# A hybrid trunk in split float32r products: first products on x as loaded, one weight tile of the opening instead of two, and an earlier low part ahead of the up tiles

## The chip, the cores and the metric

One core of one Trainium2 chip. The metric is the device time of one execution in microseconds (us); below, the median of three runs is given beside the one execution that the hardware profiler recorded. Engines: PE (TensorE, the products), DVE (VectorE), ACT (ScalarE), POOL (GpSimd) and SP, whose queue issues most transfers.

## The reference, cut to what matters

One layer on 512 rows of 1024 columns:

```
u    = x * rsqrt(mean(x*x, axis=-1) + eps) * g          # rmsnorm, g = ln1_g
proj = u @ w_in       # q, k, v, pool_in, z, xbc, dt_raw, gate_pre
y_b  = pool_mixer(pool_in): per channel, windows w = 2, 4, 8, 16 by group
       (cumsum(p)[t] - cumsum(p)[t-w]) / min(t+1, w) - p[t], then a product
x    = x + (gates * (attention, pool, state-space branches)) @ w_o
x    = x + conv_ffn(rmsnorm(x, ln2_g))                  # w_up, conv, silu, w_down
out  = rmsnorm(x, final_g)
```

The factor rsqrt(...) is one number per row of x, so it can be applied to x before a product or to the rows of the result after it.

## The kernel before, in words

**Products.** Every large product is made of three float32r products: each operand is held as a high part (rounded to float32r) and a low part (what the rounding left), and high by high (HH), high by low (HL) and low by high (LH) are added in one PSUM bank. `mm3` (its product is L239) writes them. A weight tile is 1024 rows by 256 columns: `fetch` loads it, `cast` (L195, ACT) writes the high part `wh`, `low` (L217, DVE) the low part `wl`. For the activations the two parts are `uh` and `ul`, transposed: eight tiles k of 128 columns of x, each 128 partitions by 512 rows of x. The rows of x come in four blocks of 128 (tb = 0 to 3), loaded in two halves each.

**Order of work.** Everything is issued in program order on each engine. `program()` yields a list of jobs, one weight tile each: first the eight pool column blocks (four tiles, called w0 to w3 here), then the v columns, q and k, and so on to `w_o`, the up tiles and the down tiles. Before the body of job n, `prepare` issues low(n+1), cast(n+2) and fetch(n+3); a job marked `late` calls `prepare` itself, inside its body. `step()` advances generators in the lists `running` and `waiting`, one piece of side work at each call.

**The opening** (L1814 to L1952) is written out by hand. PE runs 12 products of ones (L1833) while x is on its way. For row blocks 0 and 1, ACT and DVE form sums of squares (L442), then a chain of small operations (L1897 to L1902) ends in a diagonal matrix that holds the row factors (L1903); PE multiplies each 128x128 block of x by it (L1891), which transposes and norms in one product. ACT (L1862) and DVE (L1863) read the PSUM result, multiply by g and write `uh` and `ul` in pieces of 128x256. Row blocks 2 and 3 are normed in place (L1927, L1929) and transposed against the unit matrix `eye` later (L1940). `begin` (L1866 to L1881) does w0 and w1 in two passes: rows 0 to 255 for both tiles, then rows 256 to 511 for both, 192 products of 256 columns (L1874) in all. Between the passes stand the transposes and a transpose of small constants, `colp` (L508). From w2 on a job does 48 products of 512 columns.

**Pool evacuation** (`pool_evac`, L896 to L919). For each of the eight pool column blocks ACT copies PSUM to `pu`, POOL adds shifted copies until the window is reached (L904 to L907), and two steps later DVE subtracts `pu` (L913), ACT rounds (L915) and DVE writes the low part (L916).

**Into the FFN.** The last `w_o` job, `four`, is late: its `prepare`, which holds the low part of up tile 0, the cast of up tile 1 and the fetch of up tile 2, is put on `late_split` and run only after row block 3 of the second norm has been set up (L1325). The first two up tiles run `up_jobs.opening` (L1532 to L1562): rows 0 to 255 first, HH, HL, then transposes of the next normed block (L454), the low part of the next tile, then LH (all L1543).

## Time and profile before

| | |
|---|---|
| runs | 1013.71, 1014.82, 1015.12 us; median 1014.82 |
| profiled execution | 1014.97 us |
| its span | 1013.2 us |
| PE busy | 1001.3 us (99%), 5360 matmul records |
| DVE busy | 733.4 us (72%) |
| ACT busy | 529.9 us (52%) |
| POOL busy | 156.2 us (15%) |
| last PE product ends | 1005.85 us |

The busy time of an engine is counted inside the span; the profiled execution is 1.8 us longer than its span. Idle time of an engine counts only where another waits for it, and with PE busy 99% of the span there is very little idle time on PE: 4.58 us ahead of its last product. In rows of the trace a group reads as start, length, engine, line, operation, output<-inputs, shape, count, and in brackets the idle time ahead of it and who ended it.

### The profile page before, as it was taken

To read this page: it belongs to the slowest core of one execution; us is meant where nothing else is said; L and a number is where in the kernel's file an instruction comes from. 1 tells how busy PE (TensorE), PEld (TensorE's weight loads), DVE (VectorE), ACT (ScalarE), POOL (GpSimd) and SP (SyncE) were. 2 spreads that over 40 slices of the span, in tenths; PEclk is the share of its full clock that TensorE was granted. 3 is DMA by queue.
4 is the path that set the end of the run, shared out by engine and by line. 5 is a ranking of instruction groups with operands and counts; after the bars stand their busy time and mean duration, and the time that the engine had idled before them with its cause. 6 is when DMAs were issued, how large, how long until landed. Compare 5 with 4: busy or idle time off the path is not lost.

```text
span 1013.2 us, 13676 instructions
## 1 busy us (share of the span) xinstructions
PE 1001.3 (99%) x5360; PEld 853.5 (84%) x5360; DVE 733.4 (72%) x923; ACT 529.9 (52%) x904; POOL 156.2 (15%) x143
## 2 busy tenths in 40 slices
PE   8999999999999999999999999999999999999997
PEld 8898878999988888888888888898888888888885
DVE  6564758577767655776789888768778768685877
ACT  5433556464436566788576246554444434443455
POOL 1680010110000000000044501302111100121132
PEclk9999999999999999999999999999999999999999
DMA  7334270654352435552254754232252134542573
GB/s 238 89 102 139 84 208 5 167 169 144 99 166 76 116 94 146 142 132 62 83 149 119 222 188 87 83 123 87 89 202 84 44 115 149 181 115 73 146 181 110
DMA packets 117584, 126.76 MB, mean 125 GB/s; under 512 B 6772, under 2 KB 96439, under 8 KB 117520
## 3 DMA queue, kind: packets, MB, share of 16 engines
q1 hardware_dynamic: 111887, 116.39, 37.0%
q0 software_dynamic: 5040, 8.65, 5.5%
q8 instruction: 42, 0.69, 0.3%
q10 hardware_dynamic: 592, 0.86, 0.3%
q14 instruction: 23, 0.18, 0.1%
HBM read 121.30 MB, written 3.00 MB: 123 GB/s over the span
## 4 chain that ended last, share of the span: by engine, by line
PE 93%; DVE 3%; issue 1%; DMA 1%; ACT 1%; POOL 0%; ACTq 0%; POOLq 0%
PE pa L239 36%; PE pu L239 23%; PE pb L239 8%; PE pqk L239 6%; PE pd L239 6%; PE pq L239 3%; PE pa L1874 2%; PE ps L781 1%; PE ppw L239 1%; PE po L829 1%; DVE wl L217 1%; PE pt L815 1%; PE py L1114 1%; PE pu L1543 1%; DMA xin<-in_x_dram 1%
## 5 line engine op out<-in xcount | busy, mean ns | idle before, releaser
L217 DVE TENSOR_TENSOR wl<-raw,wh 128x2048 fp32r<-128x2048 f32 (+3 forms) x86 | 205.9, 2394 | 42.3 <-ACT wh L195 33.9
L195 ACT CAST wh<-raw 128x1024 fp32r<-128x1024 f32 (+3 forms) x169 | 169.8, 1022 | 48.6 <-DVE raw L362 17.8
L1440 DVE SCALAR_TENSOR_TENSOR hc<-pu,fcol,hc 128x510 f32<-128x510 f32 x88 | 65.8, 748 | 53.1 <-ACT hc L1437 51.4
L239 PE MATMUL pa<-uh,wh 128*128 128x512 f32 (+1 forms) x368 | 88.8, 381 | 0.0
L239 PE MATMUL pa<-ul,wh 128*128 128x512 f32 (+1 forms) x368 | 86.8, 375 | 0.0
L239 PE MATMUL pa<-uh,wl 128*128 128x512 f32 (+1 forms) x368 | 86.8, 375 | 0.0
L239 PE MATMUL pu<-uh,wh 128*128 128x512 f32 (+1 forms) x352 | 83.5, 379 | 0.0
L239 PE MATMUL pu<-uh,wl 128*128 128x512 f32 (+1 forms) x352 | 83.5, 379 | 0.0
L239 PE MATMUL pu<-ul,wh 128*128 128x512 f32 (+1 forms) x352 | 83.5, 379 | 0.0
L239 PEld LDWEIGHTS pa<-ul,wh 128*128 128x128 f32 x368 | 66.7, 188 | 12.6
L239 PEld LDWEIGHTS pa<-uh,wl 128*128 128x128 f32 x368 | 66.7, 188 | 12.5
L239 PEld LDWEIGHTS pa<-uh,wh 128*128 128x128 f32 x368 | 65.3, 188 | 11.8
L239 PEld LDWEIGHTS pu<-uh,wl 128*128 128x128 f32 x352 | 64.2, 188 | 12.5
L239 PEld LDWEIGHTS pu<-ul,wh 128*128 128x128 f32 x352 | 64.2, 188 | 12.5
L239 PEld LDWEIGHTS pu<-uh,wh 128*128 128x128 f32 x352 | 64.1, 188 | 12.4
L1445 POOL TENSOR_TENSOR hc<-hc 128x512 f32<-128x512 f32 x22 | 29.9, 1361 | 279.3 <-DVE hc L1440 243.3
L1437 ACT ACTIVATE hc<-pu,fcol,fcol 128x512 f32<-128x512 f32 x40 | 31.2, 780 | 75.0 <-PE pu L239 75.0
L217 DVE TENSOR_TENSOR wl<-w,wh 128x2048 fp32r<-128x2048 f32 (+1 forms) x26 | 54.3, 2087 | 10.2 <-issue 4.6
L195 ACT CAST wh<-w 128x1024 fp32r<-128x1024 f32 (+1 forms) x52 | 47.2, 950 | 9.8 <-DMA w<-in_ffn_w_down_dram 5.0
L803 ACT ACTIVATE sb<-sb,nmls 128x128 f32<-128x128 f32 (+1 forms) x72 | 30.0, 418 | 31.4 <-DVE nmls L800 20.8
L1097 POOL TENSOR_TENSOR st<-st,dts 128x512 f32<-128x512 f32 x4 | 4.2, 1052 | 226.1 <-ACT st L1105 165.7
L1442 ACT ACTIVATE hc<-hc 128x512 f32<-128x512 f32 x22 | 13.9, 632 | 40.3 <-DVE hc L1440 40.3
(443 smaller groups left out, 1969.4 us busy)
## 6 DMA issues: line engine op xcount, KB each, us to landing
raw<-in_w_in_dram SPq DMA_DIRECT2D x24, 1024.0 KB, 5.5
raw<-in_ffn_w_up_dram SPq DMA_DIRECT2D x22, 1024.0 KB, 5.2
raw<-in_w_in_dram SPq DMA_DIRECT2D x14, 512.0 KB
raw<-in_w_in_dram SPq DMA_DIRECT2D x8, 768.0 KB, 7.4
raw<-in_ffn_w_down_dram SPq DMA_DIRECT2D x6, 1024.0 KB, 5.1
raw<-in_w_b_dram SPq DMA_DIRECT2D x4, 1024.0 KB, 5.3
al<-ad SPq DMA_DIRECT2D x16, 256.0 KB, 6.4
raw<-in_w_c_dram SPq DMA_DIRECT2D x4, 1024.0 KB, 7.7
```

The lines of the kernel that those rows point to most:

```text
L195: (other.tensor_copy if other and i else act.copy)(job.high[:, :, o], job.raw[:, :, o])
L217: (eng or dve).tensor_tensor(l[:, :, o], job.raw[:, :, o], h[:, :, o].bitcast(F32), OP.subtract)
L239: pe.matmul(ps, l, r, start=first and n == 0, stop=last and n == total - 1, skip_group_check=onto)
L781: pe.matmul(pss[i][:, o:o + w * P], q[r, n * P:(n + 1) * P], k[r, kb * P:(kb + w) * P], start=True, stop=True)
L803: act.activation(sb[:, off:off + w * P], sb[:, off:off + w * P], AF.Exp, bias=nm[:, n, h:h + 1], accum_out=ls[:, n, h:h + 1])
L815: pe.transpose(pt[:, o:o + P], sb[:, o:o + P], eye)
L829: pe.matmul(po[DH * hh:DH * hh + DH, n * P:(n + 1) * P], V[g, kb + i][:, (2 * c + hh) * DH:(2 * c + hh + 1) * DH], probs[2 * c + hh, nb][: ...
L1437: act.activation(t, ps, AF.Identity, bias=ff["c1"][:, ff["b"] + m:ff["b"] + m + 1], scale=fw(2, m))
L1440: dve.scalar_tensor_tensor(t[:, sh:], ps[:, :S - sh], fw(k, m), t[:, sh:], OP.mult, OP.add)
L1442: act.activation(t, t, AF.Silu)
L1445: pool.tensor_tensor(a, a, t, OP.mult)
L1874: pe.matmul(first[2 * n + j][:, lo:hi], a[:, k, j * P:(j + 1) * P], b[:, k, lo:hi], start=a is wh and b is uh and k == 0, stop=a is wl and ...
```

## The change

- x is transposed as it was loaded (PE against `eye`, L1902), without the row factor. ACT (L1906) and DVE (L1907) multiply by g and write high and low parts `xh`, `xl` in 32 pieces each of 128x128. Row block 1 goes to three PSUM banks (`uT1`, `first[2]`, `first[1]`) instead of sharing those of row block 0.
- Ten products of ones stand ahead (`WARM`), seven more (`STILL`) behind the transposes of row block 1.
- Only w0 is done by hand, again in passes of 256 rows: 96 products (L1918). Its high part is cast by DVE and ACT, its low part made by POOL. w1 is an ordinary job of 48 products of 512 columns (L239).
- The row factors of all four blocks are formed during this, as a column `rcol`; PE transposes it (L1992), DVE copies it out, and it goes to DRAM and comes back as a tile `rows` with the 512 factors in every partition.
- `pool_evac` runs on DVE: a multiply by `rows` (L929), two running sums with `tensor_tensor_scan` (the first w columns at L931; then at L932 each new element adds p[t] and subtracts p[t-w]), the factor for the first w elements (L933); the difference and the low part follow four and five steps later (L938, L942). POOL no longer adds shifted copies.
- The normed `uh`, `ul` of the later jobs come from `xf`, the sum of both parts of x, times `rows` (POOL, L642), rounded by ACT (L643) and subtracted by DVE (L649). The v columns use `xh` and `xl` and ACT multiplies their results by `rcol`. Four additions on DVE (L408) are not needed any more.
- x, `eye`, g and w0 are loaded in another order; `turn()` and `parts_of_bias()` are moved three and four steps into the job loop.
- `four` is no longer late, so low(up tile 0), cast(up tile 1) and fetch(up tile 2) go ahead of its body. In the opening of up tile 0, LH now goes ahead of the transposes and of low(up tile 1); for up tile 1 the order stays.

```diff
-        f = []
-        for k in (2 * p, 2 * p + 1):
-            f.append(T("uf"))
-            dve.tensor_tensor(f[-1], uh[:, k, :].bitcast(F32), ul[:, k, :].bitcast(F32), OP.add)
+        if p < 2:
+            f = [xf[2 * p], xf[2 * p + 1]]
...
+    def normed():
+        for k in range(0, KD, 2):
+            for i in (k, k + 1):
+                pool.tensor_tensor(xf[i], xf[i], rows["r"], OP.mult)
+                act.copy(uh[:, i, :], xf[i])
+            yield
+        yield
+        for k in range(0, KD, 2):
+            yield
+            for i in (k, k + 1):
+                dve.tensor_sub(ul[:, i, :], xf[i], uh[:, i, :].bitcast(F32))
...
-            act.copy(t[:, :384], ps[:, :384])
+            act.mul(t[:, :384], ps[:, :384], rcol[:, tb:tb + 1])
...
-        return jobs_b(parts, 384 + extra, lambda k, tb: uh[:, k, tb * P:(tb + 1) * P],
-                      lambda k, tb: ul[:, k, tb * P:(tb + 1) * P], KD, evac)
+        return jobs_b(parts, 384 + extra, lambda k, tb: xh[k][:, tb * P:(tb + 1) * P],
+                      lambda k, tb: xl[k][:, tb * P:(tb + 1) * P], KD, evac)
...
-        act.copy(u, ps)
-        cur, sh = u, 1
-        while sh < w:
-            nxt = T("psw")
-            pool.tensor_tensor(nxt[:, sh:], cur[:, sh:], cur[:, :S - sh], OP.add)
-            pool.tensor_copy(nxt[:, :sh], cur[:, :sh])
-            cur, sh = nxt, sh * 2
-        pool.tensor_tensor(cur[:, :w], cur[:, :w], ramp[:, g, :w], OP.mult)
+        dve.tensor_tensor(u, ps, rows["r"], OP.mult)
+        cur = T("psw")
+        dve.tensor_tensor_scan(cur[:, :w], ones.bitcast(F32)[:, :w], u[:, :w], 0.0, OP.mult, OP.add)
+        dve.tensor_tensor_scan(cur[:, w:], u[:, w:], u[:, :S - w], cur[:, w - 1:w], OP.add, OP.subtract)
+        dve.tensor_tensor(cur[:, :w], cur[:, :w], ramp[:, g, :w], OP.mult)
         def later():
+            for _ in range(4):
+                yield
+            dve.scalar_tensor_tensor(cur, cur, 1.0 / w, u, OP.mult, OP.subtract)
+            dh, dl = T("pdh", F32R), T("pdl", F32R)
+            act.copy(dh, cur)
             yield
-            yield
-            d = T("pd")
-            dve.scalar_tensor_tensor(d, cur, 1.0 / w, u, OP.mult, OP.subtract)
-            dh, dl = T("pdh", F32R), T("pdl", F32R)
-            act.copy(dh, d)
-            dve.tensor_sub(dl, d, dh.bitcast(F32))
+            dve.tensor_sub(dl, cur, dh.bitcast(F32))
...
                 late.append(rest())
-                for _ in late_split.pop(0):
-                    pass
...
-        four.late, inner = True, four.body
-        def body(ws):
-            late_split.append(four.prepare(later=True))
-            inner(ws)
-        four.body = body
...
                 product(ws[0], uh2, 0)
                 product(ws[0], ul2, 1)
+                if half == 0:
+                    product(ws[1], uh2, 2)
                 next(late.pop(0), None)
                 next(rest[0], None)
-                product(ws[1], uh2, 2)
+                if half:
+                    product(ws[1], uh2, 2)
...
-        yield from jobs_a(w_in, C_POOL, 8, uhk, ulk, KD, pool_evac)
+        yield from jobs_a(w_in, C_POOL, 8, xhk, xlk, KD, pool_evac)
...
-    load_x(0, (sp, act))
-    act.dma_start(eye, c_eye)
-    load_x(1, (sp, act))
     act.dma_start(g8[:KD, :P], ln1_g[0].rearrange("(k p) -> k p", p=P))
+    sp.dma_start(eye, c_eye)
+    load_x(0, (act, sp))
...
+    first = [MM("pa") for _ in range(3)]
...
+    load_x(1)
+    load_w0(0, 0, 8)
+    load_w0(1, 0, 8)
     load_x(2)
     load_x(3)
+    fetch(w1)
...
-    for tb in range(2):
-        s0, s1, v, sq, r, rt = (small(n, [P, 1]) for n in ("s0", "s1", "v", "sq", "r", "rt"))
-        squares(act, xin[tb, 0], s0)
-        squares(dve, xin[tb, 1], s1)
-        dve.tensor_scalar(v, s0, 1.0 / D, EPS, OP.mult, OP.add)
...
-        if tb == 0:
-            for k in range(KD):
-                turn_scale(0, k)
+    def block(tb, k):
+        if tb == 1:
+            return (uT1, first[2], first[1])[k % 3][:, (k // 3 + 1) * P:(k // 3 + 2) * P]
+        return bank(k)[:, tb % 2 * P:tb % 2 * P + P]
+    def turned(tb):
+        if tb % 2 == 0:
+            banks[:] = [SM("uT") for _ in range(4)]
+        for k in range(KD):
+            pe.transpose(block(tb, k), xin[tb, k // 4][:, (k % 4) * P:(k % 4 + 1) * P], eye)
+    def split_x(tb, k):
+        c = slice(tb * P, (tb + 1) * P)
+        act.mul(xh[k][:, c], block(tb, k), g1[:, k:k + 1])
+        dve.scalar_tensor_tensor(xl[k][:, c], block(tb, k), g1[:, k:k + 1],
+                                 xh[k][:, c].bitcast(F32), OP.mult, OP.subtract)
...
+    warm_up(WARM)
     pe.transpose(first[2][:, :KD], g8[:KD, :P], eye[:KD, :KD])
+    turned(0)
     dve.tensor_copy(g1, first[2][:, :KD])
...
-    cast(weights[0], 2, other=dve)
-    low(weights[0], 2, pool)
     for k in range(KD):
-        turn_scale(1, k % 2 * 4 + k // 2)
+        split_x(0, k)
+    turned(1)
     for k in range(KD):
-        turned(k, 0, bank(k))
...
-    ss = row_squares(2, small("ss", [P, 4]), 2)
-    next(parts)
-    r = rstd_of(ss, 2, D)
-    for tb in (2, 3):
-        for h in range(2):
-            t = xin[tb, h]
-            if h:
-                dve.tensor_scalar(t, t, r[:, tb - 2:tb - 1], None, OP.mult)
-            else:
-                act.mul(t, t, r[:, tb - 2:tb - 1])
-    next(parts)
-    begin(0, 0, 256)
...
-    begin(1, 0, 256, turns)
-    turn()
-    parts_of_bias()
+        if k == 2:
+            for k0 in (0, 4):
+                dve.tensor_copy(h0[part(0, k0, k0 + 4)], raw0[part(0, k0, k0 + 4)])
+            low0(0, 0, KD)
+        split_x(1, k)
+    warm_up(STILL, 0)
+    group(0, (HH,), 0, 256)
+    group(0, (HL,), 0, 256)
+    for k0 in (0, 4):
+        act.copy(h0[part(1, k0, k0 + 4)], raw0[part(1, k0, k0 + 4)])
+    low0(1, 0, KD)
+    half_squares(act, 0, 0)
+    half_squares(act, 1, 0)
+    half_squares(dve, 0, 1)
+    group(1, (HH,), 0, 256)
+    turned(2)
+    for k in range(KD):
+        split_x(2, k)
+    group(1, (HL,), 0, 256)
+    group(0, (LH,), 0, 256)
+    half_squares(act, 2, 0)
+    half_squares(dve, 1, 1)
+    for k in range(KD):
+        pool.tensor_tensor(xf[k][:, :256], xh[k][:, :256].bitcast(F32), xl[k][:, :256].bitcast(F32),
+                           OP.add)
+    turned(3)
+    for k in range(KD):
+        split_x(3, k)
+    group(1, (LH,), 0, 256)
     fetch(weights[2])
+    half_squares(act, 3, 0)
+    half_squares(act, 3, 1)
+    half_squares(dve, 2, 1)
+    both_high(256, S, (0, 1))
+    group(0, (LH,), 256, S)
+    group(1, (LH,), 256, S)
+    w1.high = whp.tile([P, KD, 256], F32R, name="wh", tag="wh")
+    dve.tensor_tensor(ss[:, :4], ss[:, :4], ss[:, 4:], OP.add)
+    r = rstd_of(ss[:, :4], 4, D)
+    for j in range(2):
+        act.copy(w1.high[:, :, j * P:(j + 1) * P], w1.raw[:, :, j * P:(j + 1) * P])
+    dve.tensor_copy(rcol, r)
+    pe.transpose(first[2][:4, :P], rcol, eye)
+    rt, rd = T("rowsT"), dram.tile([S], F32, name="rows")
+    dve.tensor_copy(rt[:4, :P], first[2][:4, :P])
+    rows["r"] = T("rows")
+    sp.dma_start(rd.rearrange("(t p) -> t p", p=P), rt[:4, :P])
+    sp.dma_start(rows["r"], rd.partition_broadcast(P))
+    low(w1, 2)
+    cast(weights[2], 2)
     fetch(weights[3])
-    begin(0, 256, S)
-    cast(weights[2])
+    for k in range(KD):
+        act.mul(xf[k][:, 256:], bank(k), g1[:, k:k + 1])
     low(weights[2])
-    begin(1, 256, S)
-    cast(weights[3])
-    fetch(weights[4])
+    running.append(after(3, columns_of(turn)))
+    running.append(after(4, columns_of(parts_of_bias)))
+    for j in range(2):
+        pool_evac(j, first[j])
+        step()
+    running.append(normed())
...
-        if n >= 2:
+        if n >= 1:
...
-                    if n + 1 < len(weights):
+                    if n + 1 < len(weights) and not weights[n + 1].split:
...
-WARM = 12
+WARM, STILL = 10, 7
```

What PE runs first, before; `uT` is the PSUM bank of transposed x, `pa` a bank of products:

```order
L1833 MATMUL pa<-ones 128x128 x12
L1891 MATMUL uT<-diag,xin 128x128 x8
L1907 MATMUL pa<-eye,g_109 128x8
L1891 MATMUL uT<-diag,xin 128x128 x8
L1874 MATMUL pa<-uh,wh 128x256 x6
L1874 MATMUL pa<-ul,wh 128x256 x2
```

And after, with `uT_123` the new bank and `xh`, `xl` the parts of x as loaded:

```order
L1854 MATMUL pa<-ones 128x128 x10
L1943 MATMUL pa<-eye,g_110 128x8
L1902 MATMUL uT<-eye,xin 128x128 x8
L1902 MATMUL uT_123<-eye,xin 128x128
L1902 MATMUL pa<-eye,xin 128x128 x2
...
L1854 MATMUL pa<-ones 128x128 x7
L1918 MATMUL pa<-xh,wh 128x256 x8
L1918 MATMUL pa<-xl,wh 128x256 x8
L1918 MATMUL pa<-xh,wh 128x256 x8
L1902 MATMUL uT<-eye,xin 128x128 x8
L1918 MATMUL pa<-xl,wh 128x256 x8
L1918 MATMUL pa<-xh,wl 128x256 x8
```

The ones and the transposes follow one another without the products with `diag`, eight products of w0 run in one group (HH of the first 128 columns) ahead of any low part, and the transposes of row blocks 2 and 3 stand as two groups of eight among the products.

DVE, from the low part of w3 on, before (`pd` and `pdl` are the window difference and its low part):

```order
L217 TENSOR_TENSOR wl<-raw,wh 128x2048
L913 SCALAR_TENSOR_TENSOR pd<-psw,pu 128x512
L916 TENSOR_TENSOR pdl<-pd,pdh 128x512
L913 SCALAR_TENSOR_TENSOR pd<-psw,pu 128x512
L916 TENSOR_TENSOR pdl<-pd,pdh 128x512
```

And after, from the row factors to the first evacuated block (`psw` holds the running sum; order prints a scan as SCALAR_TENSOR_TENSOR):

```order
L1991 COPY rcol<-r_446 128x4
L1994 COPY rowsT<-pa 4x128
L217 TENSOR_TENSOR wl<-raw,wh 128x8x128 x2
L217 TENSOR_TENSOR wl<-raw,wh 128x2048
L929 TENSOR_TENSOR pu<-pa,rows 128x512
L931 SCALAR_TENSOR_TENSOR psw<-ones,pu 128x2
L932 SCALAR_TENSOR_TENSOR psw<-pu,psw 128x510
L933 TENSOR_TENSOR psw<-psw,ramp 128x2
```

DVE now evacuates each pool block itself, behind the low parts of w1 and w2, with one multiply on PSUM, two scans and a small factor.

PE at the opening of the up tiles, before (`pu` is the bank of the up products, `u_5939` a row block of the second norm):

```order
L1543 MATMUL pu<-uh_5804,wh 128x256 x16
L1543 MATMUL pu<-ul_5805,wh 128x256 x16
L454 MATMUL uT<-eye,u_5939 128x128 x4
L454 MATMUL uT<-eye,u_5940 128x128 x4
L1543 MATMUL pu<-uh_5804,wl 128x256 x16
L1543 MATMUL pu<-uh_5804,wh 128x256 x16
```

And after:

```order
L1560 MATMUL pu<-uh_5788,wh 128x256 x16
L1560 MATMUL pu<-ul_5789,wh 128x256 x16
L1560 MATMUL pu<-uh_5788,wl 128x256 x16
L457 MATMUL uT<-eye,u_5930 128x128 x4
L457 MATMUL uT<-eye,u_5931 128x128 x4
L1560 MATMUL pu<-uh_5788,wh 128x256 x16
L1560 MATMUL pu<-ul_5789,wh 128x256 x16
```

The 16 products on `wl` now stand ahead of the two groups of transposes. On DVE at the same place, before, with `x` the residual row blocks 2 and 3, `va`, `vo` scalars of their norm and `wl` the low part of up tile 0:

```order
L1352 TENSOR_TENSOR x_5529<-x_5529,pb 128x512
L1304 TENSOR_SCALAR va_102<-so_101 128x1
L1305 TENSOR_SCALAR vo_103<-va_102 128x1
...
L479 SCALAR_TENSOR_TENSOR u_5939<-x_5529,rt,grow 128x512
L1352 TENSOR_TENSOR x_5531<-x_5531,pb 128x512
L1304 TENSOR_SCALAR va_105<-so_104 128x1
L1305 TENSOR_SCALAR vo_106<-va_105 128x1
L217 TENSOR_TENSOR wl<-raw,wh 128x2048
```

And after:

```order
L217 TENSOR_TENSOR wl<-raw,wh 128x2048
L1376 TENSOR_TENSOR x_5513<-x_5513,pb 128x512
L1330 TENSOR_SCALAR va_103<-so_102 128x1
L1331 TENSOR_SCALAR vo_104<-va_103 128x1
...
L482 SCALAR_TENSOR_TENSOR u_5930<-x_5513,rt,grow 128x512
L1376 TENSOR_TENSOR x_5515<-x_5515,pb 128x512
L1330 TENSOR_SCALAR va_106<-so_105 128x1
L1331 TENSOR_SCALAR vo_107<-va_106 128x1
```

The low part of up tile 0 went from behind the second addition to ahead of the first.

More of the change, by code (lines that the diff above doesn't have):

```diff
@@ new lines, in columns_of, with mm, group @@
+    def columns_of(turn):
+        turn()
+        return
+        yield
+    opened = set()
+    def mm(j, w, b, k, lo, hi, last=False):
+        pe.matmul(first[j][:, lo:hi], w[:, k, j * P:(j + 1) * P], b[k][:, lo:hi],
+                  start=j not in opened, stop=last, skip_group_check=True)
+        opened.add(j)
+    def group(j, pairs, lo, hi, ks=range(KD)):
+        for w, b in pairs:
+            for k in ks:
+                mm(j, w, b, k, lo, hi, w is l0 and k == KD - 1)
+    HH, HL, LH = (h0, xh), (h0, xl), (l0, xh)
```

100 lines of the change are left out of this document (43 added, 57 removed).

## The prediction

> **What bounds the kernel now.** I read the totals and the chain's shares on the page first, then the chain of waits of the first 60 us, then what PE waited for, then the rows of the two places that are edited.
>
> ```profile
> PE 1001.3 (99%) x5360; PEld 853.5 (84%) x5360; DVE 733.4 (72%) x923; ACT 529.9 (52%) x904; POOL 156.2 (15%) x143
> PE 93%; DVE 3%; issue 1%; DMA 1%; ACT 1%; POOL 0%; ACTq 0%; POOLq 0%
> ```
>
> PE bounds the kernel: it is busy 99% of the span. Time can come from four things only: PE starting its real work earlier, fewer or cheaper products, shorter waits of PE, a shorter tail. The change touches the first three. The chain shows what the opening consists of:
>
> ```profile
> 1.67 6.58 DMA xin<-in_x_dram
> ...
> 10.04 0.36 DVE diag L1903
> ...
> 10.44 2.05 PE uT L1891 x16
> 12.49 9.60 PE pa L1874 x80
> 22.09 1.75 PE uT L1940 x16
> 23.84 1.92 PE pa L1874 x16
> 25.75 0.12 issue
> 25.88 0.27 PE colp L508
> 26.14 11.54 PE pa L1874 x96
> 37.68 21.79 PE pa L239 x96
> ```
>
> The last piece of x lands at 8.25, a chain of small operations ends in `diag` at 10.40, and only then can PE finish the first transposes. From 12.25 it runs without a gap, and w1 ends at 37.68. The prices on PE come from here: a product of 256 columns 11.54/96 = 0.120, one of 512 columns 21.79/96 = 0.227, a transpose 1.75/16 = 0.109. Check: 192 × 0.120 + 1.75 + 0.4 from 12.3 on gives 37.5.
>
> PE's waits before the tail are few; three are at the two places:
>
> ```profile
> PE uT L1891 <- DVE diag L1903: 2.2, 2, 1.2
> PE pa L1833 <- DVE ones L1824: 1.1, 1, 1.1
> PE pu L1543 <- DVE wl L217: 1.0, 1, 1.0
> ```
>
> **The change, the opening.** PE waits for no row factor now; what its products need is `xh`, and for that the pace of ACT and DVE counts. The 32 pieces of 128x128 are no form of before, so I take them from these rows:
>
> ```profile
> 23.22 3.04 ACT L1862 ACTIVATE uh<-uT,g 128x256 fp32r<-128x256 f32 x8 [1.51 <-PE uT L1940]
> 23.73 3.22 DVE L1863 SCALAR_TENSOR_TENSOR ul<-uT,g,uh 128x256 fp32r<-128x256 f32 x8 [1.40 <-ACT uh L1862]
> L1862 ACT ACTIVATE uh<-uT,g 128x256 fp32r<-128x256 f32 x16 | 6.3, 486 | 2.4 <-PE uT L1940 1.5 <-PE uT L1891 0.9
> L930 ACT ACTIVATE ybh<-ppw,col 128x512 fp32r<-128x512 f32 x8 | 5.5, 689 | 7.1 <-PE ppw L239 7.1
> L1863 DVE SCALAR_TENSOR_TENSOR ul<-uT,g,uh 128x256 fp32r<-128x256 f32 x16 | 6.6, 477 | 2.0 <-ACT uh L1862 2.0
> L1127 DVE SCALAR_TENSOR_TENSOR xs<-xs,dgc,ea 128x128 f32<-128x128 f32 x24 | 6.8, 348 | 0.2
> ```
>
> Eight pieces of 256 columns follow each other on ACT every (3.04 − 0.49)/7 = 0.36, on DVE every 0.39. From 512 to 256 columns ACT saves 689 − 486 = 203 ns, so from 256 to 128 half of that, 0.10 us; DVE saves 477 − 348 ns = 0.13 us. That makes 0.26 on both. Bounds: 0.18 if the pace halves with the columns, and 0.36 if a piece is as dear as one of 256. I take 0.26, from the row of equal width.
>
> The clock enters through the ones:
>
> ```profile
> 1.06 4.95 PE L1833 MATMUL pa<-ones 128*128 128x128 f32 x24 [1.06 <-DVE ones L1824]
> ...
> 1.00:5.06 4.06, 4.00 (x18) 4.00 (x19) 1.00 0.75 222
> 5.06:6.00 0.94, 0.94 (x7) 0.75 (x6) 1.00 1.09 340
> ```
>
> Each ones product leaves two records. Up to 5.06 a record takes 4.06/19 = 0.21, behind it 0.11 or less: PE gets fast at about 5, after 4 us of work, though the granted clock in the row reads 1.00 in both. Ten products end at 1.06 + 20 × 0.21 = 5.3. The transpose of g and its copy to `g1` end near 5.8, and from there ACT sets the pace: row block 0 takes 8 × 0.26 and ends at 7.9. In row block 1 DVE does two pieces to 8.85, then two casts of half of w0's first 128 columns, 512 elements each, 0.37 each by half of this row:
>
> ```profile
> 10.38 0.68 DVE L195 CAST wh<-raw 128x1024 fp32r<-128x1024 f32 x1
> 11.14 4.77 POOL L217 TENSOR_TENSOR wl<-raw,wh 128x1024 fp32r<-128x1024 f32 x2 [10.69 <-DVE wh L195]
> ```
>
> So DVE goes on at 9.6. With three banks ACT's piece k waits for DVE's piece k − 3 of the same bank, and its last three follow DVE: ACT ends at 10.85, and HH of w0's first half, eight products that take `xh` piece by piece, ends at 11.0. The low parts on POOL, 2.4 each, are ready at 12.0 and about 14.4 and wanted at 14.7 and 16.6: covered.
>
> From 11.0 PE is dense: 96 − 8 = 88 products × 0.120 = 10.6, 16 transposes 1.75, the transpose of `rcol` 0.15: w0 ends at 23.5. w1 as a job takes 48 × 0.227 = 10.9, the moved `colp` 0.2: 34.6, against 37.68. **Term 1: −3.1.** Of it 48 × (2 × 0.120 − 0.227) = 0.65 is the wider product; the rest, 2.4, is the earlier start. ACT's two casts for w1 come after the last squares, near 22.7, wanted at 23.5: the smallest cover here; if it is gone, each 0.1 counts whole.
>
> **The row vector and the evacuations.** `rowsT` is written near 23.7; out to DRAM and back costs two transfers, and a broadcast from DRAM took 3.9 at 256 KB:
>
> ```profile
> b<-rdram SPq DMA_DIRECT2D x3, 256.0 KB, 3.9
> ```
>
> With a write no longer than that it lands by 31.5 at the latest, 28 as I expect; PE wants a bank back from the first evacuation at 34.6. Hidden. SP has the fetch of w3 behind these two transfers, so near 26.5; in 5.5 us or twice that it is there before the cast for PE's 45.5. POOL needs `rows` for eight multiplications before `uh` is read near 75:
>
> ```profile
> L1445 POOL TENSOR_TENSOR hc<-hc 128x512 f32<-128x512 f32 x22 | 29.9, 1361 | 279.3 <-DVE hc L1440 243.3
> ```
>
> At this row's price they take 10.9 of the 40 us, and ACT's eight roundings 5.5: hidden too. DVE now carries what ACT and POOL did. Between 28.4 and the end of w3 on PE at 34.6 + 21.8 = 56.4 it has 28.0 us. Its queue there, besides seven evacuations:
>
> ```profile
> L217 DVE TENSOR_TENSOR wl<-raw,wh 128x2048 fp32r<-128x2048 f32 x6 | 13.8, 2308 | 10.2 <-ACT wh L195 10.2
> L217 DVE TENSOR_TENSOR wl<-raw,wh 128x1600 fp32r<-128x1600 f32 x2 | 4.5, 2232 | 0.0
> L338 DVE TENSOR_TENSOR sal<-sa,sah 128x512 fp32r<-128x512 f32 x19 | 13.0, 683 | 2.2 <-PE po L829 2.2
> L951 DVE SCALAR_TENSOR_TENSOR xs<-pa,col,xs 128x510 f32<-128x510 f32 x8 | 6.0, 749 | 0.3
> L866 DVE RECIPROCAL dtmp<-den 6x512 f32<-6x512 f32 x1 | 3.3, 3332 | 0.0
> ```
>
> Two low parts 2.3 + 2.2, five window differences or low parts at 0.7, small copies 1.2: 9.2. An evacuation is a multiply (0.7), two small operations (0.4) and the scan. So the queue keeps up while a scan stays under (28.0 − 9.2)/7 − 1.1 = 1.6. No scan stands in this trace: 0.75 if it costs as an operation of 510 columns (L951), 3.3 if as the slowest row of that length (L866). I take 1.16, half as much again as the nearer row. After w3 the last `ul` is done at 56.4 + 18.8 (evacuation 2.3, two low parts 4.5, eight `ul` 5.5, eight differences or low parts 5.5, two copies 1.0) = 75.2; the products of q and k that read it come 3.1 earlier than here:
>
> ```profile
> 79.65 1.98 PE L239 MATMUL pqk<-ul,wh 128*128 128x512 f32 x8
> ```
>
> There the reading begins at 79.65 − 3.1 = 76.5 and reaches the last tile near 78. **Term 2: 0**, with some 2.8 to spare for the last tile. [...]
>
> **The up tiles.** Rows of before, on DVE:
>
> ```profile
> 656.45 0.68 DVE L1352 TENSOR_TENSOR x<-x,pb 128x512 f32<-128x512 f32 x1
> ...
> 659.57 0.68 DVE L1352 TENSOR_TENSOR x<-x,pb 128x512 f32<-128x512 f32 x1
> 660.42 2.28 DVE L217 TENSOR_TENSOR wl<-raw,wh 128x2048 fp32r<-128x2048 f32 x1
> ...
> 665.82 2.28 DVE L217 TENSOR_TENSOR wl<-raw,wh 128x2048 fp32r<-128x2048 f32 x1
> ```
>
> and on PE:
>
> ```profile
> 660.75 1.04 PE L454 MATMUL uT<-eye,u 128*128 128x128 f32 x8
> 662.75 2.18 PE L1543 MATMUL pu<-uh,wl 128*128 128x256 f32 x16 [0.97 <-DVE wl L217]
> ...
> 669.40 2.15 PE L1543 MATMUL pu<-uh,wl 128*128 128x256 f32 x16
> ```
>
> The low part of up tile 0 (here the one at 660.42) now runs at 656.45 instead of 660.42, so LH follows HL at 660.75 without the 0.97. But both additions of x, and the norms behind them, stand 2.28 later on DVE. The first transposes, now behind LH, still find their block. The low part of up tile 1 is put behind the norm of the last block and one pair of `ul`: by adding those rows it ends at 668.95, and PE would want it at 669.40 − 0.97 − 0.1 = 668.35 (behind its wait the group of 16 took 2.02, the others 1.92). A new wait of 0.6 takes the place of the one removed: PE starts that LH at 669.0 instead of 669.40. **Term 3: −0.4**; bounds 0 and −0.97.
>
> The cast moved up with it costs ACT the same, only earlier, and SP's queue gets one fetch earlier; neither is waited for by PE in the rows around it. The tail and all between are the same rows.
>
> **Sum** against the profiled execution: 1014.97 − 3.1 − 0.4 = 1011.5. The median of the runs shown is 0.15 lower: 1011.4.
>
> **The rivals.**
> (a) *The small pieces are dear.* At 0.36 a piece the 16 of the two first row blocks take 16 × 0.10 = 1.6 longer, ahead of all PE work: 1013.0. For it: the pieces of 256 columns do cost 0.36 in a row. Against: the row of 128 columns.
> (b) *The clock.* From 5.3 to 11.0 PE has only transposes, seven ones and eight products that come one by one. If that is not enough to stay fast, about 30 products and transposes at 0.21 to 0.24 instead of 0.11 to 0.12 cost 30 × 0.11 = 3.3: 1014.7, no change, and the earlier start is given back. For it: the slow records up to 5.06. Against: in before PE is fast at 12.25 although it idled 0.99 and 1.24 and did mostly transposes since 6. [...]
> (c) *DVE becomes the bound.* Eight evacuations stand on DVE that ACT and POOL did before. If a scan costs s, DVE is late at the end of w3 by 7 × (s − 1.6), longer by s − 1.16 for the eighth, and has 2.8 to spare: PE waits for the last `ul` from s = 1.9 on. As dear as the reciprocal, 3.3: 11.9 + 2.1 − 2.8 = 11.2 more: 1022.6, slower. For it: a scan hands each element to the next. Against: the nearest row is 0.75.
> (d) *More than I count.* The pieces overlap better than in lockstep, and the whole 0.97 is won: 1010.2.
> (e) *It does not do what it says:* w1's cast arrives late by what its 0.8 of cover lacks, and the gap eats part of the start: up to 1 us of term 1, counted in the forecast's own range.
>
> **How the numbers follow.** Forecast 0.60 (1010.0 to 1012.6 by itself), (a) 0.14, (b) 0.11, (c) 0.10, (d) 0.05. A measurement of this kernel can tell about 0.2%, 2.0 us, from no change: the band is 1012.8 to 1016.8. Faster holds the forecast, (d) and nearly half of (a), 0.71; the same holds the rest of (a) and (b), 0.19; slower is (c), 0.10. The range leaves out (c), half of (d) and a little of (b): 1009.8 to 1014.6.
>
> **What would show it.** w1's last product ends near 34.6; the first product of w0 starts before 9 and its eight end near 11.0, at 0.120 from then on (slower: rival b); the pieces at L1906 and L1907 cost 0.26 apart (0.36: rival a); a scan at L932 stays under 1.9 and no PE row of w2, w3, v or q waits for DVE (else rival c); PE's wait of 0.97 at the first up tile is gone and one of about 0.6 stands at the second; everything after 75 us is shifted by 3.1 up to 656 and by 3.5 behind 669. The forecast is wrong if PE has a new wait behind 11 us that is longer than 1, above all for w1's cast at 23.5 or for `rows` at 34.6.

## The result, and the profile after

The changed kernel takes 1012.99 us (median of 21 runs, 1012.30 to 1013.91), the kernel before 1014.21 (21 runs, 1013.59 to 1015.57) in the same comparison: a ratio of 0.9987, with a 95% interval of 0.9981 to 0.9993. That is 1.2 us less, between 0.7 and 1.9: faster beyond the interval, but inside the 0.2% within which the prediction counted a change as none. The prediction was 1011.4, 3.4 less than the median of three runs it went by, with a range up to 1014.6. In what follows one run, of the kernel open_only, took 3562.96 us; it is not in that kernel's ratio.

The two profiled executions stand 2.4 us apart (spans 1013.2 and 1010.8). There are therefore two questions: where the predicted 3.4 went, and why the profiles differ by more than the medians. The chain of waits of the changed kernel, up to w2:

```profile
1.36 4.20 DMA xin<-in_x_dram
...
5.61 0.78 PE uT L1902 x5
...
6.41 0.38 ACT xh L1906
...
6.81 2.68 DVE xl L1907 x10
9.49 0.67 DVE wh L1952 x2
10.16 0.27 DVE xl L1907
...
10.46 0.38 ACT xh L1906
...
10.88 2.80 PE pa L1918 x19
13.68 0.87 PE uT L1902 x8
14.55 1.91 PE pa L1918 x16
16.46 1.19 PE uT L1902 x8
17.65 6.71 PE pa L1918 x56
24.36 0.11 PE pa L1992
24.47 10.92 PE pa L239 x48
35.38 0.08 PE colp L511
35.46 21.82 PE pa L239 x96
```

The chain shows the lockstep: ten pieces of `xl` on DVE at 0.268 each, its two casts, then one more `xl` that releases ACT's `xh`, which releases PE. From 10.88 on only PE stands in the chain. w2 begins at 35.46; before it began at 37.68, and 34.6 was forecast. What PE waits for in the whole program:

```profile
PE pa L1854 <- DVE ones L1843: 1.1, 1, 1.1
PE pa L1918 <- ACT xh L1906: 0.8, 1, 0.8
PE pu L1560 <- DVE wl L217: 0.6, 1, 0.6
PE uT L1902 <- DMA xin<-in_x_dram: 0.5, 1, 0.5
```

The wait at the first up tile is gone and one of 0.6 stands at the second, as forecast. No row of w2, w3, v or q waits for DVE. PE's last product ends at 1002.94 (1005.85 before), 2.9 earlier. Of the 2.9, 2.2 is the earlier w2 and 0.7 lies between w2 and the last product. The span is only 2.4 shorter, so behind the last product something has become longer, by 0.5.

### The profile page after: what moved, and what is told of

It reads as the page before. It is cut to its first block, busy times and chain, and to the rows that moved or that the text cites. A ratio compares the mean times of both kernels' runs of the same rounds, so it can differ in the third digit from the quotient of the medians.

```text
span 1010.8 us, 13607 instructions
## 1 busy us (share of the span) xinstructions
PE 999.7 (99%) x5307; PEld 850.0 (84%) x5307; DVE 753.7 (75%) x962; ACT 534.7 (53%) x929; POOL 137.8 (14%) x111
## 4 chain that ended last, share of the span: by engine, by line
PE 96%; DVE 2%; ACT 0%; DMA 0%; issue 0%; ACTq 0%
PE pa L239 37%; PE pu L239 23%; PE pb L239 10%; PE pd L239 8%; PE pqk L239 6%; PE pq L239 3%; PE ps L810 1%; PE pa L1918 1%; PE ppw L239 1%; PE po L858 1%; PE pt L844 1%; PE py L1140 1%; DVE wl L217 1%; PE pyo L1147 1%; PE pst L1128 0%; DMA xin<-in_x_dram 0%
## 5 line engine op out<-in xcount | busy, mean ns | idle before, releaser
L195 ACT CAST wh<-raw 128x1024 fp32r<-128x1024 f32 (+2 forms) x168 | 167.0, 1011 | 53.0 <-DVE raw L362 17.8
L239 PE MATMUL pu<-uh,wh 128*128 128x512 f32 (+1 forms) x352 | 83.6, 379 | 0.0
L239 PE MATMUL pu<-uh,wl 128*128 128x512 f32 (+1 forms) x352 | 83.5, 379 | 0.0
L239 PE MATMUL pu<-ul,wh 128*128 128x512 f32 (+1 forms) x352 | 83.5, 379 | 0.0
L239 PE MATMUL pa<-uh,wh 128*128 128x512 f32 (+1 forms) x336 | 80.9, 380 | 0.0
L239 PE MATMUL pa<-ul,wh 128*128 128x512 f32 (+1 forms) x336 | 78.9, 374 | 0.0
L239 PE MATMUL pa<-uh,wl 128*128 128x512 f32 (+1 forms) x336 | 78.8, 374 | 0.0
L239 PEld LDWEIGHTS pu<-ul,wh 128*128 128x128 f32 x352 | 64.2, 188 | 12.5
L239 PEld LDWEIGHTS pu<-uh,wl 128*128 128x128 f32 x352 | 64.2, 188 | 12.4
L239 PEld LDWEIGHTS pu<-uh,wh 128*128 128x128 f32 x352 | 64.1, 188 | 12.4
L239 PEld LDWEIGHTS pa<-ul,wh 128*128 128x128 f32 x336 | 60.7, 188 | 11.4
L239 PEld LDWEIGHTS pa<-uh,wl 128*128 128x128 f32 x336 | 60.7, 188 | 11.2
L239 PEld LDWEIGHTS pa<-uh,wh 128*128 128x128 f32 x336 | 59.4, 189 | 10.6
```

Source lines behind the costliest of these rows:

```text
L195: (other.tensor_copy if other and i else act.copy)(job.high[:, :, o], job.raw[:, :, o])
L239: pe.matmul(ps, l, r, start=first and n == 0, stop=last and n == total - 1, skip_group_check=onto)
```

## The experiments

All times that carry a ratio were taken beside runs of the kernel before on the same chip. The median of before was 1014.06 to 1014.44 in these comparisons, so times from different ones are compared by their ratios. The columns: start of w2 on PE; from PE's last product to the end of the span (the tail); both from one profiled execution.

| kernel | w2 starts | tail | time, us | ratio to before, 95% |
|---|---|---|---|---|
| before, three executions | 37.68, 36.77, 37.38 | 7.35, 7.35, 7.34 | 1014.21 | |
| changed, two executions | 35.46, 35.73 | 7.83, 7.82 | 1012.99 | 0.9987 (0.9981 to 0.9993) |
| open_only | 35.29 | 7.83 | 1013.03 | 0.9985 (0.9977 to 0.9994) |
| up_only | 37.37 | 7.34 | 1013.92 | 0.9996 (0.9988 to 1.0005) |
| pad_pool | 36.14 | 7.49 | 1012.88 | 0.9984 (0.9975 to 0.9992) |
| x_first | 36.79 | 7.79 | 1012.76 | 0.9985 (0.9976 to 0.9993) |
| cast_pool | 34.82 | 7.96 | 1012.00 | 0.9978 (0.9968 to 0.9987) |
| no_still | 35.69 | 7.82 | 1012.75, one run | |
| no_ones | 36.76 | 7.80 | 1014.23 | 0.9996 (0.9987 to 1.0005) |
| norm_dve | 35.37 | 7.51 | 1012.10, one run | |
| cast_pad | 34.42 | 7.50 | 1011.83 | 0.9978 (0.9969 to 0.9988) |

**Further executions of both kernels** (before_look, before_look2, after_look: no edit).

> A second look at the kernel before, unchanged. The two profiled executions differ by 2.4 us, the medians by 1.2. Theory A: the first profiled execution of before was one in which x landed late (8.25), so the opening of before is usually shorter: here the last piece of x lands earlier than 8.25, the first product of w0 starts earlier than 12.25 by as much, and w1 ends before 37.68. Theory B: the opening repeats within 0.1 us and executions differ only behind PE's last product (7.35 us from it to the end of the span), in the last transfer. Under A the true worth of the new opening is near 1.0, under B it is the 2.2 that the two profiles show and the tail hides it.

> A second look at the changed kernel, unchanged. Theory A: its opening waits for the first half of x only and then for ACT and DVE, so the end of w1 repeats at 35.4 within 0.2 us. Theory B: the same, but the stretch behind PE's last product differs from 7.8 us by up to 1.

> A third look at the kernel before. In the two looks so far the last piece of x landed at 8.25 and 7.33 and the first product of w0 came at 12.25 and 11.33; the medians are explained if it usually comes near 11.5. Expected: between 11.0 and 12.3, the end 7.35 behind PE's last product again.

Measured: the chain of the second and the third execution of the kernel before, to the products of w2.

```profile
9.52 2.05 PE uT L1891 x16
11.57 9.59 PE pa L1874 x80
...
25.22 11.55 PE pa L1874 x96
36.77 21.79 PE pa L239 x96
```

```profile
1.67 6.28 DMA xin<-in_x_dram
...
10.14 2.05 PE uT L1891 x16
12.20 9.59 PE pa L1874 x80
...
25.85 11.54 PE pa L1874 x96
37.38 21.79 PE pa L239 x96
```

The last piece of x landed at 7.33 and 7.95 instead of 8.25, and w2 begins 0.9 and 0.3 earlier, at the same prices. Theory A holds for the opening: the execution that the prediction rested on was the latest of the four that have this opening (up_only began w2 at 37.37). Theory B falls in the form in which it was put: the tail does not vary from one execution to the next. It repeats within 0.01, and it is 7.34 to 7.35 with the old opening and 7.82 to 7.83 with the new one in the changed kernel and open_only. That was in neither theory: the tail differs by kernel, by 0.48.

Executions also differ ahead of the last product. From the start of w2 to PE's last product the three of before take 968.17, 968.63 and 967.77, the two of the changed kernel 967.48 and 967.46. The first two of before lose time among the last down products: 0.3 near 1002 in the first, 0.6 near 996 and 0.2 near 1002 in the second. The rows of the second near 996:

```profile
993.06 1.29 POOL L1618 TENSOR_TENSOR xg<-x,grow 128x512 f32<-128x512 f32 x1 [0.29 <-DVE x L1674]
993.18 2.79 DVE L217 TENSOR_TENSOR wl<-w,wh 128x1536 fp32r<-128x1536 f32 x1 [0.20 <-ACT wh L195]
996.71 0.93 PE L239 MATMUL pb<-wh,sbh 128*128 128x512 f32 x3 [0.38 <-DVE x L1674]
```

In the third execution DVE's `wl` begins at 993.48, just ahead of POOL's `xg` at 993.64; there `wl` takes 1.75 and PE does not wait. So the 2.4 between the two first profiles is 2.2 from the opening (0.4 of it by the late x), 0.3 from the up tiles, 0.3 from the wait near 1002 in before and 0.1 that is spread out, less 0.5 in the tail.

**The two parts apart.**

```diff
 open_only: the changed kernel with
+                for _ in late_split.pop(0):
+                    pass
...
+        four.late, inner = True, four.body
+        def body(ws):
+            late_split.append(four.prepare(later=True))
+            inner(ws)
+        four.body = body
...
-                if half == 0:
-                    product(ws[1], uh2, 2)
                 next(late.pop(0), None)
                 next(rest[0], None)
+                product(ws[1], uh2, 2)

 up_only: the kernel before with the opposite of these lines
```

> The changed kernel with the up opening put back as it was (the job four late, LH behind the transposes). If the terms add, PE waits 0.97 again at the first up tile and nothing at the second, the opening is as in the changed kernel (w1 ends near 35.4), and the time is 0.35 above the changed kernel: a ratio to before of 0.9991 if the opening is worth what the medians leave (0.9 us), 0.9980 if it is worth the 2.2 that the two profiles show.

> The kernel before with the new up opening alone. If the terms add, the wait of 0.97 at the first up tile goes, one of about 0.6 stands at the second, and the time falls by 0.35 us: ratio 0.9997, within the interval of no change. The rival, that the earlier low part collides with something else, would show as a new wait of PE between 640 and 680 us and a ratio over 1.

Measured: PE at the two first up tiles, in up_only and then in open_only.

```profile
660.41 2.08 PE L1534 MATMUL pu<-uh,wl 128*128 128x256 f32 x16
662.33 1.04 PE L454 MATMUL uT<-eye,u 128*128 128x128 f32 x8
...
668.70 2.17 PE L1534 MATMUL pu<-uh,wl 128*128 128x256 f32 x16 [0.63 <-DVE wl L217]
```

```profile
658.27 1.04 PE L457 MATMUL uT<-eye,u 128*128 128x128 f32 x8
660.31 2.18 PE L1569 MATMUL pu<-uh,wl 128*128 128x256 f32 x16 [1.00 <-DVE wl L217]
...
666.96 2.15 PE L1569 MATMUL pu<-uh,wl 128*128 128x256 f32 x16
```

The wait moves from the first tile to the second and shrinks by a third of a microsecond with either opening: from 0.97 to 1.00 in the four executions with the old up tiles to 0.63 to 0.68 in those with the new ones. By time, the up part alone gains 0.4 us, which its interval cannot tell from nothing; the opening alone is 0.9985. In the profiles the terms add and no new wait stands between 640 and 680; the intervals of the times are too wide to show it. The tail follows the opening: 7.34 in up_only, 7.83 in open_only.

**What the tail is: pad_pool.**

```diff
     act.activation(warm, warm, AF.Sqrt)
+    pad = cpool.tile([P, 1], F32, name="pad")
+    for _ in range(31):
+        pool.memset(pad, 0.0)
```

> The changed kernel with 31 small memsets on POOL at its start, where POOL is idle till 10.24, so that POOL has as many instructions as before (229 instead of 198 in the trace). Behind PE's last product the two versions of before took 7.35 and 7.34 us, those of after 7.82 and 7.83; 0.30 of that stands on POOL between its last drain and its next semaphore operation (0.35 instead of 0.04). Theory A (where POOL's program ends decides, by its length): the gap goes back to 0.04, the tail to about 7.5, and the time falls by 0.3 us, ratio to before 0.9985. Rival B (the tail is set by the output's landing or by what else the new opening uses): the gap on POOL stays 0.35 and the tail 7.8.

Measured, from the instruction records of POOL's last lines (us behind PE's last product: last drain, next semaphore operation, end of the span):

```
before     7.08   7.17   7.35
changed    7.25   7.64   7.83
open_only  7.24   7.64   7.83
pad_pool   7.22   7.31   7.49
cast_pool  7.56   7.78   7.96
norm_dve   7.24   7.33   7.51
cast_pad   7.24   7.32   7.50
```

The step from the drain to the semaphore operation takes 0.39 in the changed kernel and 0.08 in pad_pool, as before. So 0.30 of the longer tail hangs on POOL's instructions, which do nothing there but close the program. In cast_pool, with one instruction more, the lost time stands ahead of the drain. A longer program is not a quicker one as a rule: 229 (before, up_only, pad_pool), 228 (cast_pad) and 182 (norm_dve) are quick, while 198 (the changed kernel) and 199 (cast_pool) are slow. The DMA records differ in the same way: all seven executions with the lost time have an instruction transfer of 8 KB behind the last instructions, and none of the seven without the loss has it. But that transfer starts 8.25 to 8.57 behind the last product, after the end of the span, so it does not show what fills the 0.3. The other 0.17 stayed with the padding: SP, at the program's end, waits for the transfers one after another, in another order than before. The last transfer lands at 6.22 to 6.24 in either kernel; in before SP comes to it last, at 6.45, in the changed kernel earlier in its list, and six more waits of 0.06 follow. By time pad_pool (0.9984) cannot be told from the changed kernel (0.9987); its profiled execution also had a late opening.

**What sets the start: x_first, cast_pool.**

```diff
 x_first
-    act.dma_start(g8[:KD, :P], ln1_g[0].rearrange("(k p) -> k p", p=P))
     sp.dma_start(eye, c_eye)
     load_x(0, (act, sp))
+    act.dma_start(g8[:KD, :P], ln1_g[0].rearrange("(k p) -> k p", p=P))
...
-    pe.transpose(first[2][:, :KD], g8[:KD, :P], eye[:KD, :KD])
     turned(0)
+    pe.transpose(first[2][:, :KD], g8[:KD, :P], eye[:KD, :KD])

 cast_pool
-                dve.tensor_copy(h0[part(0, k0, k0 + 4)], raw0[part(0, k0, k0 + 4)])
+                pool.tensor_copy(h0[part(0, k0, k0 + 4)], raw0[part(0, k0, k0 + 4)])
```

> The changed kernel with g loaded behind the first half of x on ACT's queue, and its transpose behind those of row block 0. Theory: the opening is late because the first half of x lands at 5.57 instead of 4.62; then x lands near 5.0, the first xh is at 5.9 instead of 6.41, w1 ends near 34.9 instead of 35.4, and the time falls by 0.5 us. Rival: g lands as late as x did, g1 gates the first xh, and nothing moves (35.4).

> The changed kernel with the two casts of w0's first half on POOL instead of DVE. Theory (the lockstep of ACT and DVE over three banks sets the opening): DVE's chain is 0.67 shorter, the last xh starts at 10.3 instead of 10.98, the first eight products end near 11.0 instead of 11.6, w1 ends near 34.8. Rival: a POOL cast costs as much as POOL's subtraction (1.2 for 512 elements), the second cast ends behind 10.5 and the products on it are as late as now or up to 1 us later (w1 ends at 35.4 to 36.4).

x_first measured the rival or worse in its profile. The transposes start at 5.48, straight behind the ones, but take 0.21 each, since PE was still slow; g is copied at 7.54, the first `xh` comes at 7.75, and w2 at 36.79. This execution, 1013.89, stands 1.1 above the median of its 11 runs, so it is no fair picture of the kernel. In time the kernel is the same as the changed one, 0.9985 against 0.9987. So the gain of 0.5 that I had put on the landing of x did not show; what that landing is worth with a fast PE stays open.

cast_pool measured the theory. ACT and POOL there:

```profile
6.37 2.43 ACT L1906 ACTIVATE xh<-uT,g 128x128 fp32r<-128x128 f32 x9 [3.12 <-PE uT L1902]
...
10.27 0.36 ACT L1906 ACTIVATE xh<-pa,g 128x128 fp32r<-128x128 f32 x1
...
9.16 1.17 POOL L1952 CAST wh<-raw 128x512 fp32r<-128x512 f32 x2 [8.71 <-DMA raw<-in_w_in_dram]
```

ACT began as in the changed kernel (6.37 against 6.41) and its last piece starts at 10.27 instead of 10.98, since DVE no longer stands still for the casts. A cast of 512 elements costs POOL 0.6, not the 1.2 of its subtraction. w2 begins at 34.82, 0.64 earlier, and the time is 1012.00; its ratio 0.9978 against 0.9987 points the same way, but the intervals overlap. What PE waits for now is `wh` from POOL (0.7), and POOL for w0's landing.

**What the ones are worth: no_still, no_ones.**

```diff
-WARM, STILL = 10, 7
+WARM, STILL = 10, 0        (no_still)
+WARM, STILL = 0, 0         (no_ones)
```

> The changed kernel without the seven products of ones behind the transposes of row block 1, so that PE idles from 7.4 to 10 with nothing but transposes ahead. Theory A (PE keeps its speed over such a pause): the products from 10 on come at 0.12, w1 ends at 35.4 and the time is as with them. Rival B (the clock is lost): the first products behind the pause take 0.24 each until some 4 us of work have passed, w1 ends 2 to 3 us later, near 38.

> The changed kernel without any product of ones: PE begins with the transposes near 5.5. In the looks so far PE's pitch fell from 0.213 to 0.11 at 3.9 to 7.3 us, another moment in each execution, after ones from 1.06 on. Theory A (PE must have worked for some time before it becomes fast): it is slow until 8 to 11 us, the transposes take 0.2 each and part of the first products 0.24; w1 ends 1 to 3 us later than 35.5. Rival B (the moment is fixed from the start of the program and does not depend on work): the pitch falls at 4 to 7 us here too and nothing is lost.

Measured: PE in no_still, where it idles 2.4, and in no_ones.

```profile
10.19 1.80 PE L1918 MATMUL pa<-xh,wh 128*128 128x256 f32 x8 [2.40 <-ACT xh L1906]
11.83 1.11 PE L1918 MATMUL pa<-xl,wh 128*128 128x256 f32 x8
```

```profile
5.39 2.18 PE L1902 MATMUL uT<-eye,xin 128*128 128x128 f32 x9 [2.24 <-DMA xin<-in_x_dram]
...
10.38 2.05 PE L1918 MATMUL pa<-xh,wh 128*128 128x256 f32 x8 [1.31 <-ACT xh L1906]
12.22 1.80 PE L1918 MATMUL pa<-xl,wh 128*128 128x256 f32 x8
13.86 1.11 PE L1918 MATMUL pa<-xh,wh 128*128 128x256 f32 x8
```

no_still keeps its speed: the second group of eight follows at 0.95 for eight products, w2 is at 35.69, and the time of its one run is like the changed kernel's. In the execution seen, the seven ones bought nothing. no_ones is slow to 13.7: the transposes take 0.21 each, the first 16 products 0.21 instead of 0.12, and w2 begins at 36.76. Theory A holds for the ten ones: in the profile they are worth 1.1 to 1.3 us. By time they are worth 0.9, the difference of the ratios, which is about what the whole change gains; the two intervals overlap by a little.

**DVE's load: norm_dve.**

```diff
-                pool.tensor_tensor(xf[i], xf[i], rows["r"], OP.mult)
+                dve.tensor_tensor(xf[i], xf[i], rows["r"], OP.mult)
```

> The changed kernel with the eight multiplications of x by the row factors on DVE instead of POOL. In the changed kernel the first three scans of 508 to 510 columns take 2.27, the later ones 1.26, and a multiply of 2 columns 1.07 instead of 0.17; POOL is at work until 41.8. Theory A (POOL's work beside them slows these DVE operations): with POOL idle all eight scans take 1.26 and the small operations 0.17; DVE wins back some 5 us for the 5.4 that it takes over, and PE has no new wait. Rival B (the scans of 508 and 510 columns are slow by their form or because the factors have just landed): the first three stay at 2.27, DVE is 5.4 us longer, and PE waits for the last low part of u near 76 by 3 us or more.

Measured: the scans and the multiply beside them, first in the changed kernel, then here (the last numbers are busy us and mean ns).

```profile
L929 DVE TENSOR_TENSOR pu<-pa,rows 128x512 f32<-128x512 f32 x8 | 5.5, 682 | 0.5 <-DMA rows<-rows 0.5
L932 DVE TENSOR_TENSOR_SCAN psw<-pu,psw 128x510 f32<-128x510 f32 x2 | 4.6, 2279 | 0.1
L932 DVE TENSOR_TENSOR_SCAN psw<-pu,psw 128x508 f32<-128x508 f32 x2 | 3.5, 1769 | 0.1
L932 DVE TENSOR_TENSOR_SCAN psw<-pu,psw 128x496 f32<-128x496 f32 x2 | 2.5, 1252 | 0.1
L933 DVE TENSOR_TENSOR psw<-psw,ramp 128x2 f32<-128x2 f32 x2 | 2.1, 1070 | 0.1
```

```profile
L932 DVE TENSOR_TENSOR_SCAN psw<-pu,psw 128x510 f32<-128x510 f32 x2 | 2.6, 1280 | 0.1
L932 DVE TENSOR_TENSOR_SCAN psw<-pu,psw 128x508 f32<-128x508 f32 x2 | 2.6, 1276 | 0.1
L933 DVE TENSOR_TENSOR psw<-psw,ramp 128x2 f32<-128x2 f32 x2 | 0.3, 161 | 0.1
```

In the changed kernel POOL multiplies from 29.88 to 41.76, and the three scans of that time take 2.26 to 2.29; a mean of 1.77 is one of them and one behind it. With POOL idle every scan takes 1.25 to 1.28 and the multiply of 2 columns 0.16. Theory A holds: POOL's work cost these DVE operations up to a whole microsecond each. The last `ul` ends at 75.5 instead of 76.9, although DVE does more. PE waits for neither, so no time comes of it.

**Both edits that moved something: cast_pad** (cast_pool with 29 of the memsets).

> The changed kernel with both edits that moved something: the casts of w0's first half on POOL (w1 0.6 earlier in the profile, time 0.9 lower) and 29 small memsets ahead on POOL, so that POOL has 229 instructions as before. If the two add, the stretch behind PE's last product falls from 7.96 (casts alone) to 7.5, w1 ends near 34.7, and the time is 1011.6 to 1011.9: ratio to before 0.9975. Rival: the place at which POOL's last instructions fall depends on more than their count, the gap stays, and the time is that of the casts alone, 1012.0.

Measured: w2 at 34.42, the tail 7.50, 1011.83 us, ratio 0.9978 (0.9969 to 0.9988). It is the fastest version here and beats before by 2.2 us (1014.06 in this comparison); against the changed kernel that is some 0.9 more, by the ratios of two comparisons. Whether the memsets add to the casts its interval does not tell (0.9978 too); the tail, 7.50 against 7.96, shows that they do. That w2 begins 0.4 before cast_pool's is not shown to be their work: w0 landed at 8.58 here and at 9.10 there.

## Why the prediction was right in kind and too large

**Term 1, the opening, −3.1.** This is the step that failed, in its size. By w2's start, the four executions with the old opening average 37.30; the six with the new one (changed twice, open_only, norm_dve, pad_pool, and no_still, which lacks the seven ones) 35.61: −1.7. Of the 1.4 that are missing, 0.4 is the reference and 1.0 the new opening:

- *The reference.* 37.68 was one execution, with x at 8.25. Since before waits for the last piece of x and the changed kernel does not, that landing counts whole in the difference. This took 0.4 from the term. I had noted that the profiled execution stood only 0.15 above the median of three runs; over 21 runs it was 0.76, to which its late wait near 1002 may add 0.3.
- *"From there ACT sets the pace", near 5.8.* In the six executions the first `xh` came at 6.23 to 7.04, 6.55 on average: 0.75 of the 1.0. The step went from the copy of g straight to ACT and left out what the transposes wait for. In the changed kernel's first execution and in open_only that is the first half of x, which lands at 5.57 and 5.38 and for which the sum had no term; in the other four it is the ones and g's transpose, with which PE is done at 5.5 to 5.8, since it became fast later. Then ACT needs not one transpose but five, because pieces k = 0 and k = 4 of row block 0 share a bank and ACT is released by the later of them. The chain shows it as `uT` x5, 0.78 in the changed kernel. So the first product of w0, forecast before 9, came at 9.97. From the first `xh` to w2 it is 29.05 and 29.07 in the two executions of the changed kernel, where my steps give 34.6 − 5.8 = 28.8: the pitch of 0.26, the lockstep over three banks, the casts, the 88 dense products and w1's 10.92 were right within 0.3 in all.

**Term 2, row vector and evacuations, 0.** Right. The factors landed at 29.7, against 28 expected and a bound of 31.5, and no product waited. The rival that DVE becomes the bound named a scan of 1.9 as the point from which it decides; three scans, beside POOL's work, took 2.26 to 2.29, but the other five 1.25 to 1.28. The mean is 1.64, so it did not decide. No run shows the 1.16 that the sum took for a scan, an estimate from the row of 0.75: undisturbed, the scan of 510 columns took 1.28 in norm_dve, 1.7 times the 0.75 of the operation of 510 columns at L951. The last `ul` at 76.9 was read near 79: 2 to spare against 2.8 forecast.

**Term 3, the up tiles, −0.4.** Right: the wait of 0.97 is gone, one of 0.64 stands at the second tile, and the gain is 0.3 with either opening.

**The tail, 0 forecast.** "The tail and all between are the same rows": the rows are the same, but the program ends 0.48 later behind them, 0.30 on POOL, 0.17 in SP's last waits. Nothing in the profile of before shows it. What lies between is not the same from one execution to the next either, as the waits near 996 and 1002 show.

Together: −1.7 − 0.3 + 0.5 = −1.5, against −1.2 (−0.7 to −1.9) by time.

**The rivals.** (a) The pieces cost 0.26 to 0.27, not 0.36. (b) PE's speed was not lost behind the ones: no_still, in the one execution seen, kept its speed over a pause of 2.4. (d) The whole 0.97 was not won. (e) w1's cast came in time. That 1012.99 is the time named for (a) is chance, since its pieces did not cost that. The direction came with the mechanism forecast, but the time lies outside the forecast's own 1010.0 to 1012.6 and within the wider range only by the room that was left for rivals which did not happen. My 0.71 for more than 0.2% was too sure for a sum of which most hung on one landing of one execution and on a start that left out another landing.

## What to carry to other kernels

Before a gain of a few microseconds is counted at a program's start, look at two or three executions: where the old code waits for a transfer and the new one does not, the difference is as uncertain as that landing (7.33, 7.95 and 8.25 in the three executions of before). Where two engines hand pieces to each other over few banks, anything else in the queue of either (here two casts of 0.33) stands whole in the chain; put it on a third engine (with the casts on POOL, w2 began 0.64 earlier). Here a bank shared by two pieces released its reader with the later of them: five transposes, 0.78, stood ahead of the first `xh`, where one would have done.

## What the runs showed of the hardware that I had not expected

**PE became fast at another moment from one execution to the next.** The step from one record of PE to the next falls from 0.213 to 0.11; with ones from 1.06 on it fell at about these times (us), each with the start of the first product of w0 where the opening is the changed one:

```
changed 3.9 (9.97)   open_only 4.3 (9.79)   norm_dve 5.0 (9.87)   changed again 5.9 (10.22)
no_still 5.9 (10.19)   pad_pool 6.7 (10.60)   x_first 7.3 or later   before 5.3, 5.0, 6.0
up_only 5.8   cast_pool 5.1   cast_pad 4.3   no_ones 13.7
```

The granted clock reads 1.00 on both sides of the step in before, changed, pad_pool and no_ones: the column does not show this. Three stretches of no_ones (start and end, length, PE busy and its records, granted clock, then two columns of the transfers): 16 transposes at 0.22, 16 products at 0.21, then 11 records at 0.10, all at a clock of 1.00.

```profile
5.39:8.85 3.46, 3.46 (x16) 1.00 1.14 320
10.38:13.72 3.34, 3.34 (x16) 1.00 1.07 371
13.72:14.82 1.10, 1.10 (x11) 1.00 1.08 344
```

The moments with ones spread over 3.4 us or more (3.9 to 7.3 or later). The first product of w0 spreads over 0.8. Only the later moments delay it: up to 5.0 it came at 9.79 to 9.97, from 5.9 on at 10.19 to 10.60; where PE was fast at 3.9 and 4.3, it then waited 0.5 and 0.2 for x. What sets the moment is not shown. Whether transposes help to make PE fast is not settled: in no_ones 16 of them in a row from 5.39 to 8.85, at 0.22 each, did not, but a pause of 1.31 stood behind them.

**POOL's work slowed DVE operations, but not all.** Beside POOL's multiplications the scans and the small multiply, whose inputs are both in SBUF, took longer, 2.26 to 2.29 instead of 1.25 to 1.28 and 1.07 instead of 0.16 for 2 columns, while the multiply on a PSUM bank (L929) kept its 0.68 (at 34.53 and 39.21). In the two cases near 993 the one that began second was held: DVE's low part took 2.79 instead of 1.75 where POOL's multiply had begun 0.12 ahead of it (the second execution of before), and POOL's multiply 2.75 instead of 1.30 where DVE had begun 0.17 ahead (the first). Why is not shown.

**POOL's last instructions cost 0.3 us more or nothing in these runs**, with the same work (the last drain at 7.08 and the next semaphore operation at 7.17 in before, 7.25 and 7.64 in the changed kernel, 7.22 and 7.31 in pad_pool): quick with 182, 228 and 229 instructions on POOL, slow with 198 and 199. What decides is not shown.
